# Attention scores on 64 rows of the tensor engine, and the sink as a score column, in a two-layer decoder step

## The chip, the cores and the metric

The program runs on one core of a Trainium2 chip. Times are microseconds (us) of device time for one execution; the time of the kernel is the median of its runs.

## The reference, cut to what matters

One inference step of a two-layer decoder: layer 0 mixes tokens with sliding-window attention, layer 1 with gated linear attention; each is followed by a gated convolutional FFN and a layer norm. 512 prompt positions and 8 single-token samples go through together (520 columns). All arithmetic is float32. The part that the change touches is the prompt's attention of layer 0: 16 query heads, 2 key/value heads (8 query heads share one), head size 64, window 128, and a learned sink per head that takes part in the softmax but has no value:

```
scores = einsum('bnqkgd,bnskd->bnkgqs', qb, kk) * HEAD_DIM ** -0.5   # 128 queries x 256 keys a block
mask   = (kpos >= 0) & (kpos <= qpos) & (qpos - kpos < 128)
s = where(mask, scores, -1e30);  m = maximum(max(s), sink)
p = exp(s - m);  probs = p / (sum(p) + exp(sink - m));  o = probs @ vv
```

## The kernel before, in words

**Layout.** Activations lie with features on the 128 partitions and positions along the free dimension. The 520 positions form two groups, a (positions 0 to 255) and b (256 to 511 and the 8 samples). Work is a list of units, one 128x1024 weight tile each; unit 0 makes the keys, unit 1 the values, units 2 to 9 the queries (unit c+2 holds head c in partitions 0 to 63 and head c+8 in 64 to 127), then come 8 units of the output projection and the FFN. Every unit is done for group a and, some units later, for group b (`order`).

**Float32 in two parts.** TensorE multiplies in fp32r, a shortened float32. So each operand is split in a high part (ScalarE copies it to fp32r) and a low part (VectorE subtracts the high part from the original), and a product is hi*hi + hi*lo + lo*hi: three matmuls for each of 8 chunks (`product`, L164 to L166). Weights arrive by DMA in `raw` (two buffers, RAWS = 2, so a load waits until the low part wl of the load two before it is done, L152); their high part wh is made on GpSimd for the first ten units (L151) and on ScalarE after that (L149).

**Attention, one query unit of one group (`attn_q`).** After the product and the rotation (`rope`, L318 to L324) the queries are split. In `attn_k` and `attn_q` of this kernel the split is laid out for scores of 128 rows: tile `qs` holds for each of the unit's two heads (v = 0, 1) the 64 rows of the high part and, in the other 64 partitions, the 64 rows of the low part (L371, L372, 64 partitions each); the keys' high and low parts are each stored twice, in both halves (`khi[v]`, `klo[v]`, L335 to L339). So one matmul of 128 rows does qhi*khi + qlo*khi (L395) and a second adds the products with klo (L396): 2 matmuls for each head and block of 128 queries, 8 a unit. Scores go to a PSUM tile `sc` per head (two buffers).

The mask keeps for every query the lower triangle of its own block and the upper triangle of the block before, so both fit in one 128x128 square: a predicated copy puts the own block's part over the other one (L408, L412). Group a's first block has no block before it: there VectorE adds mask0 and takes the maximum in one instruction (L406). Then come the maximum (L409, L413), its negative with the sink (L415), exp(sink - m) on ScalarE (L416), the two exponentials with their sums (L418), the sum with the sink's part (L419), its reciprocal (L420), and the scaling by it, on GpSimd for v = 0 and on VectorE for v = 1 (L423). One unit later the probabilities are transposed (L429), copied (L431), split in the two triangles on GpSimd (L435), and again one unit later multiplied with the values (L445; each head takes 64 columns of TensorE).

**Order.** The instruction order of each engine's queue is fixed when the program is built, by a planner that simulates the engines; it starts from the order of the code and lets what its simulation has ready go ahead. Engines run their queues in order. The transfers of the value and key caches (`vc`, `kc`) go out in the same SyncE queue as the weights; the one for `vc` (L380) is pinned behind the weight load that stands before it in the code.

Of the kernel before, what the change touches and what calls it, by code (L numbers as in the profile page):

```python
# [11 lines left out]
F32 = mybir.dt.float32  # L12
F32R = mybir.dt.float32r
I32 = mybir.dt.int32
AF = mybir.ActivationFunctionType
ALU = mybir.AluOpType
AX = mybir.AxisListType
# [3 lines left out]
P = 128  # L21
D = 1024
KD = 8
SEQ = 512
# [12 lines left out]
NEG = -1e30  # L37
# [29 lines left out]
C_SINK = C_LNB + 4 * KD  # L67
# [22 lines left out]
class Net:  # L90
# [175 lines left out]
    def attn_open(self):  # L266
        nc, I = self.nc, self.I
        self.ap, self.ap_cm = self.open("attn")
        p = self.ap
        t = lambda s, name, dt=F32: p.tile(s, dt, name=name)  # L270
        self.rope_t = t([P, 2, NT], "rope_t")
        self.mask0 = t([P, P], "mask0")
        self.own = t([P, 2, P], "own", I32)


        warm = self.acc.tile([P, 512], F32, name="accp")
        for _ in range(WARM):
            nc.tensor.matmul(warm[:, :P], self.ones_c, self.ones_c, start=True, stop=True)
        with self.tc.manual_schedule(engines={mybir.EngineType.SP}):
            r = self.raw.tile([P, KD * P], F32, name="raw")  # L280
            h, l = (self.wts.tile([P, KD * P], F32R, name=n) for n in ("wh", "wl"))
            for m in range(0, KD, 4):
                c = slice(m * P, m * P + 4 * P)
                nc.sync.dma_start(out=r[:, c], in_=I["w_qkv"][0][:, c])
                nc.gpsimd.tensor_scalar(h[:, c], r[:, c], 1.0, 0.0, op0=ALU.mult, op1=ALU.add)
                self.load_x(0, m, m + 2)
                nc.vector.tensor_tensor(l[:, c], r[:, c], h[:, c].bitcast(F32), op=ALU.subtract)
                self.load_x(0, m + 2, m + 4)
            self.w[0] = (h, l)
            self.load_unit(1, 4)  # L290
            nc.sync.dma_start(out=self.par, in_=I["par"])
            nc.sync.dma_start(out=self.rope_t[:, :, 0:256], in_=I["rope"][:, :, 0:256])
            nc.sync.dma_start(out=self.ident, in_=I["ident"])
            self.load_unit(2, 2)
            self.load_unit(3)
            for m in range(0, KD, 4):
                self.load_x(1, m, m + 4)
            nc.sync.dma_start(out=self.rope_t[:, :, 256:], in_=I["rope"][:, :, 256:])
            nc.sync.dma_start(out=self.mask0, in_=I["mask"])
            nc.sync.dma_start(out=self.own, in_=I["own"])  # L300
            for i in range(4, WSLOTS):
                self.load_unit(i)
        self.bq = t([P, KD], "bq")
        nc.vector.tensor_scalar(self.bq, self.par[:, C_BQKV + 2:C_BQKV + 10], 0.125, None, op0=ALU.mult)
        self.khi = [t([P, SEQ], f"khi{v}", F32R) for v in range(2)]
        self.klo = [t([P, SEQ], f"klo{v}", F32R) for v in range(2)]
        self.vtok = t([P, 4, P], "vtok")
        self.kc = t([P, NS, P], "kc")
        self.vc = t([P, NS, P], "vc")
        self.qz = t([P, NS * P], "qz")  # L310
        nc.gpsimd.memset(self.qz, 0.0)
# [15 lines left out]
    def attn_k(self, g, u):  # L327
        nc = self.nc
        ps = self.product(g, u, g.xh, g.xl)
        r = self.rope(g, ps, 1.0, self.par[:, C_BQKV:C_BQKV + 1])  # L330
        cs = slice(g.c0, g.c0 + 256)
        for v in range(2):
            own = slice(64 * v, 64 * v + 64)
            oth = slice(64 - 64 * v, 128 - 64 * v)
            nc.scalar.activation(self.khi[v][own, cs], r[own, :256], AF.Copy)  # L335
            nc.scalar.activation(self.khi[v][oth, cs], r[own, :256], AF.Copy)
            hi = self.khi[v][own, cs].bitcast(F32)
            nc.vector.tensor_tensor(self.klo[v][own, cs], r[own, :256], hi, op=ALU.subtract)
            nc.vector.tensor_tensor(self.klo[v][oth, cs], r[own, :256], hi, op=ALU.subtract)  # L339
        yield 0  # L340
        if g.i:
            self.pcopy(self.kc[:, :, 127], r[:, 256:])
            nc.scalar.dma_start(out=self.O["k_prompt"], in_=r[:, 128:256])
# [19 lines left out]
    def attn_q(self, g, u, c):  # L363
        nc = self.nc
        ps = self.product(g, u, g.xh, g.xl)
        r = self.rope(g, ps, 0.125, self.bq[:, c:c + 1])
        qs = self.ap.tile([P, 2, 256], F32R, name="qs", bufs=2)
        for v in range(2):
            own = slice(64 * v, 64 * v + 64)
            oth = slice(64 - 64 * v, 128 - 64 * v)  # L370
            nc.scalar.activation(qs[own, v], r[own, :256], AF.Copy)  # L371
            nc.vector.tensor_tensor(qs[oth, v], r[own, :256], qs[own, v].bitcast(F32), op=ALU.subtract)  # L372
            if g.i:
                o = c + 8 * v
                self.pcopy(self.qz[own, o:o + 7 * 144 + 1:144], r[own, 256:])
        if g.i and c < 2:
# [7 lines left out]
        yield 1  # L384


        parts = []
        scs = [self.mtile("sc").rearrange("p (b w k) -> p b w k", b=2, w=2) for v in range(2)]
        for v in range(2):
            for b in range(2):  # L390
                n = 2 * g.i + b
                keys = slice(0, 256) if n == 0 else slice(P * (n - 1), P * (n + 1))
                o = scs[v][:, b].rearrange("p w k -> p (w k)")
                qb = qs[:, v, b * P:(b + 1) * P]
                nc.tensor.matmul(o, qb, self.khi[v][:, keys], start=True, stop=False)  # L395
                nc.tensor.matmul(o, qb, self.klo[v][:, keys], start=False, stop=True)  # L396
        prs = []
        for v in range(2):
            h = c + 8 * v
            sink = self.par[:, C_SINK + h:C_SINK + h + 1]  # L400
            sc = scs[v]
            pr = self.ap.tile([P, 2, P], F32, name="pr", bufs=4)
            small = self.ap.tile([P, 8], F32, name="small", bufs=4)
            mx, nm, es, den = (small[:, 2 * i:2 * i + 2] for i in range(4))
            if g.i == 0:
                nc.vector.tensor_tensor_reduce(pr[:, 0], sc[:, 0, 0], self.mask0, 1.0, NEG,  # L406
                                               op0=ALU.add, op1=ALU.max, accum_out=mx[:, 0:1])
                nc.vector.copy_predicated(sc[:, 1, 0], self.own[:, 0], sc[:, 1, 1])  # L408
                nc.vector.tensor_reduce(mx[:, 1:2], sc[:, 1, 0], axis=AX.X, op=ALU.max)  # L409
                src = [pr[:, 0], sc[:, 1, 0]]  # L410
            else:
                nc.vector.copy_predicated(sc[:, :, 0], self.own, sc[:, :, 1])  # L412
                nc.vector.tensor_reduce(mx, sc[:, :, 0], axis=AX.X, op=ALU.max)  # L413
                src = [sc[:, 0, 0], sc[:, 1, 0]]
            nc.vector.tensor_scalar(nm, mx, sink, -1.0, op0=ALU.max, op1=ALU.mult)  # L415
            nc.scalar.activation(es, nm, AF.Exp, bias=sink)  # L416
            for b in range(2):
                nc.scalar.activation(pr[:, b], src[b], AF.Exp, bias=nm[:, b:b + 1], accum_out=den[:, b:b + 1])  # L418
            nc.vector.tensor_tensor(den, den, es, op=ALU.add)  # L419
            nc.vector.reciprocal(den, den)  # L420
            for b in range(2):
                eng = nc.vector if v else nc.gpsimd
                eng.tensor_scalar(pr[:, b], pr[:, b], den[:, b:b + 1], 1.0, op0=ALU.mult, op1=ALU.mult)  # L423
            prs.append(pr)
        yield 1
        for pr in prs:
            tp = self.mtile("tp")[:, :256]
            for b in range(2):
                nc.tensor.transpose(tp[:, b * P:(b + 1) * P], pr[:, b], self.ident)  # L429
            pt = self.ap.tile([P, 2, P], F32, name="pt", bufs=2)  # L430
            nc.scalar.copy(pt.rearrange("p b q -> p (b q)"), tp)  # L431
            pu = self.ap.tile([P, 2, P], F32, name="pu", bufs=2)
            pl = self.ap.tile([P, 2, P], F32, name="pl", bufs=2)
            for dst, sgn, base in ((pu, 1, 0), (pl, -1, -1)):
                nc.gpsimd.affine_select(out=dst, in_=pt, pattern=[[0, 2], [sgn, P]], compare_op=ALU.is_ge,  # L435
                                        fill=0.0, base=base, channel_multiplier=-sgn)
            parts.append((pl, pu))
        yield 1
        pv = self.mtile("pv")
        for b in range(2):  # L440
            n = 2 * g.i + b
# [597 lines left out]
```

## Time and profile before

| | us |
|---|---|
| median of 3 runs (1185.88 to 1188.42) | 1185.92 |
| the profiled execution | 1187.92 |
| its span | 1185.1 |
| PE busy in the span | 1127.1 (95%) |
| VectorE busy | 777.6 (66%) |
| ScalarE busy | 556.0 (47%) |
| GpSimd busy | 362.0 (31%) |

In the profile PE is TensorE's matmuls and PEld its weight loads, DVE is VectorE, ACT ScalarE, POOL GpSimd, SP SyncE (SPq its queue of DMA issues). Matmuls are pipelined: a row's duration is longer than the distance to the next one, and a busy PE is not one at its peak. A float32 matmul that isn't fp32r shows as two rows. PEclk is the granted share of TensorE's full clock. An arrow names what ended a wait.

### The profile page before, as it was taken

How to read it: one execution, taken by the hardware profiler on the slowest of the kernel's cores; microseconds unless marked ns; L12 is line 12 of the kernel's file. 1: busy time of each engine (PE TensorE's matmuls, PEld its weight loads, DVE VectorE, ACT ScalarE, POOL GpSimd, SP SyncE). 2: the span in 40 equal slices, each digit the busy share in tenths (PEclk: the TensorE clock that was granted, in tenths of full speed). 3: DMA queues.
4: the chain of work that ended last, by engine and by line, in shares of the span. 5: the costliest groups of instructions: out<-in, count | busy, mean ns of one | idle time of the engine just before them, and what ended most of it. 6: DMA issues, size and time to landing. Idle time of an engine off the chain costs nothing.

```text
span 1185.1 us, 24433 instructions
## 1 busy us (share of the span) xinstructions
PE 1127.1 (95%) x9598; PEld 1088.0 (92%) x9598; DVE 777.6 (66%) x1649; ACT 556.0 (47%) x1222; POOL 362.0 (31%) x603
## 2 busy tenths in 40 slices
PE   8869989999999999999899999998999999999994
PEld 7768779899999999999799899898999999999994
DVE  7969878854555445558867678789645555355567
ACT  4447645643444234435555455456533443244433
POOL 5646676510011001147500000368210111011345
PEclk9989999999999999999899999999999999999997
DMA  7124013223323232332123553542323332323212
GB/s 224 58 82 138 2 27 123 72 81 116 108 90 108 90 107 90 107 118 95 54 72 95 160 174 121 169 127 90 94 85 119 95 107 90 107 90 107 73 61 72
DMA packets 49547, 118.57 MB, mean 100 GB/s; under 512 B 5753, under 2 KB 23321, under 8 KB 49433
## 3 DMA queue, kind: packets, MB, share of 16 engines
q1 hardware_dynamic: 47417, 115.41, 31.2%
q10 hardware_dynamic: 2016, 1.62, 0.4%
q8 instruction: 75, 1.23, 0.4%
q14 instruction: 39, 0.32, 0.1%
HBM read 108.54 MB, written 8.47 MB: 99 GB/s over the span
## 4 chain that ended last, share of the span: by engine, by line
PE 73%; DVE 12%; DMA 5%; POOL 4%; issue 3%; ACT 2%; SPq 0%; POOLq 0%; DVEq 0%; ACTq 0%
PE accp L165 22%; PE accp L164 22%; PE accp L166 22%; DMA raw<-in_w_qkv 2%; DMA vb<-dv 2%; DVE wl L152 2%; POOL x_b L254 1%; PE pv L445 1%; POOL x_a L254 1%; DVE u L245 1%; DVE qs L372 1%; DVE x_b L240 1%; DVE x_a L240 1%; PE sc L706 1%; PE pv L717 1%
## 5 line engine op out<-in xcount | busy, mean ns | idle before, releaser
L152 DVE TENSOR_TENSOR wl<-raw,wh 128x1024 fp32r<-128x1024 f32 (+2 forms) x189 | 229.1, 1213 | 142.1 <-ACT wh L149 131.6
L149 ACT ACTIVATE wh<-raw 128x1024 fp32r<-128x1024 f32 (+1 forms) x176 | 183.4, 1042 | 215.3 <-PE accp L165 191.8
L164 PE MATMUL accp<-xh_b,wh 128*128 128x264 f32 x976 | 273.5, 280 | 2.8 <-DVE hprod L543 2.8
L165 PE MATMUL accp<-xl_a,wh 128*128 128x256 f32 x976 | 271.4, 279 | 3.5 <-DVE xl_a L257 2.8
L166 PE MATMUL accp<-xh_a,wl 128*128 128x256 f32 x976 | 270.5, 278 | 3.0 <-DVE wl L152 3.0
L165 PE MATMUL accp<-xl_b,wh 128*128 128x264 f32 x976 | 272.8, 280 | 0.4 <-DVE xl_b L257 0.4
L164 PE MATMUL accp<-xh_a,wh 128*128 128x256 f32 x976 | 270.1, 279 | 3.2 <-ACT conv L526 1.4
L166 PE MATMUL accp<-xh_b,wl 128*128 128x264 f32 x976 | 272.1, 279 | 0.0
L165 PEld LDWEIGHTS accp<-xl_a,wh 128*128 128x128 f32 x976 | 187.7, 192 | 5.7 <-DVE xl_a L257 3.7
L164 PEld LDWEIGHTS accp<-xh_a,wh 128*128 128x128 f32 x976 | 187.1, 193 | 6.3 <-ACT conv L526 1.8
L166 PEld LDWEIGHTS accp<-xh_a,wl 128*128 128x128 f32 x976 | 188.1, 193 | 5.0 <-DVE wl L152 4.0
L164 PEld LDWEIGHTS accp<-xh_b,wh 128*128 128x128 f32 x976 | 186.7, 191 | 4.0 <-DVE hprod L543 3.2
L165 PEld LDWEIGHTS accp<-xl_b,wh 128*128 128x128 f32 x976 | 186.6, 191 | 1.9 <-issue 0.9
L166 PEld LDWEIGHTS accp<-xh_b,wl 128*128 128x128 f32 x976 | 186.1, 191 | 1.4 <-issue 1.3
L164 PE MATMUL accp<-hh_b,wh 128*128 128x264 f32 x480 | 133.4, 278 | 2.6 <-ACT hh_b L170 2.6
L165 PE MATMUL accp<-hl_b,wh 128*128 128x264 f32 x480 | 134.2, 280 | 0.0
L166 PE MATMUL accp<-hh_b,wl 128*128 128x264 f32 x480 | 133.3, 278 | 0.0
L165 PE MATMUL accp<-hl_a,wh 128*128 128x256 f32 x480 | 132.3, 276 | 0.3 <-DVE hl_a L171 0.3
L164 PE MATMUL accp<-hh_a,wh 128*128 128x256 f32 x480 | 132.2, 278 | 0.0
L166 PE MATMUL accp<-hh_a,wl 128*128 128x256 f32 x480 | 131.8, 275 | 0.0
L164 PEld LDWEIGHTS accp<-hh_b,wh 128*128 128x128 f32 x480 | 91.2, 190 | 3.1 <-ACT hh_b L170 2.9
L165 PEld LDWEIGHTS accp<-hl_a,wh 128*128 128x128 f32 x480 | 91.9, 192 | 1.3 <-issue 0.8
(304 smaller groups left out, 2095.6 us busy)
## 6 DMA issues: line engine op xcount, KB each, us to landing
raw<-in_w_up SPq DMA_DIRECT2D x88, 512.0 KB, 3.4
raw<-in_w_down SPq DMA_DIRECT2D x32, 512.0 KB, 3.5
raw<-in_w_gla SPq DMA_DIRECT2D x24, 512.0 KB, 3.5
raw<-in_w_mix_o SPq DMA_DIRECT2D x16, 512.0 KB, 3.9
raw<-in_w_down SPq DMA_DIRECT2D x16, 384.0 KB, 3.1
sgla<-in_state_gla SPq DMA_DIRECT2D x16, 256.0 KB, 2.8
vb<-dv SPq DMA_DIRECT2D x16, 256.0 KB, 3.9
out_gla_s<-sgla SPq DMA_DIRECT2D x16, 256.0 KB, 2.9
```

The costliest lines, as they stand in the source:

```text
L149: nc.scalar.activation(h[:, c], r[:, c], AF.Copy)
L152: nc.vector.tensor_tensor(l[:, c], r[:, c], h[:, c].bitcast(F32), op=ALU.subtract)
L164: nc.tensor.matmul(o, h[:, ks], xh, start=k == 0, stop=False)
L165: nc.tensor.matmul(o, h[:, ks], xl, start=False, stop=False)
L166: nc.tensor.matmul(o, l[:, ks], xh, start=False, stop=k == nt - 1)
L240: nc.vector.tensor_tensor(x[:, m], x[:, m], mu, op=ALU.subtract)
L245: nc.vector.tensor_tensor(u, x[:, m], r, op=ALU.mult)
L254: ts = nc.gpsimd.tensor_scalar(x[:, m], u, sc, bi, op0=ALU.mult, op1=ALU.add)
L372: nc.vector.tensor_tensor(qs[oth, v], r[own, :256], qs[own, v].bitcast(F32), op=ALU.subtract)
L445: nc.tensor.matmul(pv[64 * v:64 * v + 64, b * P:(b + 1) * P], self.vtok[:, kb, 64 * v:64 * v + 64], parts[v][w][:, b], start=i == 0, stop= ...
L706: nc.tensor.matmul(up, vks[b][:, 0:P], vks[b][:, P:], start=True, stop=True)
L717: nc.tensor.matmul(ob, att[:, b], vks[b][:, P:], start=first, stop=True)
```

## The change

Keys and queries are split in the plain way, 128 partitions at a time, and the keys are stored once. A score is now three matmuls of 64 rows, qhi*khi + qlo*khi + qhi*klo, where head v uses the partitions of its own half; the two heads of a unit alternate, each into its own `sc` tile. That is 12 matmuls a unit in place of 8. The sink's value is written by VectorE into the column behind the 128 masked scores, so that the maximum (now one instruction that also negates) and the exponentials with their sums take it in; the separate steps for it go. In group a's first block the mask is put in by a predicated copy in place of the add-and-maximum. The scaling of v = 1 becomes one instruction for both blocks.

```diff
-        self.khi = [t([P, SEQ], f"khi{v}", F32R) for v in range(2)]
-        self.klo = [t([P, SEQ], f"klo{v}", F32R) for v in range(2)]
+        self.khi = t([P, SEQ], "khi", F32R)
+        self.klo = t([P, SEQ], "klo", F32R)
 # attn_k
-        for v in range(2):
-            own = slice(64 * v, 64 * v + 64)
-            oth = slice(64 - 64 * v, 128 - 64 * v)
-            nc.scalar.activation(self.khi[v][own, cs], r[own, :256], AF.Copy)
-            nc.scalar.activation(self.khi[v][oth, cs], r[own, :256], AF.Copy)
-            hi = self.khi[v][own, cs].bitcast(F32)
-            nc.vector.tensor_tensor(self.klo[v][own, cs], r[own, :256], hi, op=ALU.subtract)
-            nc.vector.tensor_tensor(self.klo[v][oth, cs], r[own, :256], hi, op=ALU.subtract)
+        self.split(self.khi[:, cs], self.klo[:, cs], r[:, :256])
 # attn_q
-            nc.scalar.activation(qs[own, v], r[own, :256], AF.Copy)
-            nc.vector.tensor_tensor(qs[oth, v], r[own, :256], qs[own, v].bitcast(F32), op=ALU.subtract)
+        self.split(qh, ql, r[:, :256])
...
-                nc.tensor.matmul(o, qb, self.khi[v][:, keys], start=True, stop=False)
-                nc.tensor.matmul(o, qb, self.klo[v][:, keys], start=False, stop=True)
+            for i, (q, k) in enumerate(((qh, self.khi), (ql, self.khi), (qh, self.klo))):
+                for v in range(2):
+                    own = slice(64 * v, 64 * v + 64)
+                    nc.tensor.matmul(scs[v][:, b], q[own, b * P:(b + 1) * P], k[own, keys], start=i == 0, stop=i == 2)
...
-                nc.vector.tensor_tensor_reduce(pr[:, 0], sc[:, 0, 0], self.mask0, 1.0, NEG,
-                                               op0=ALU.add, op1=ALU.max, accum_out=mx[:, 0:1])
-                nc.vector.copy_predicated(sc[:, 1, 0], self.own[:, 0], sc[:, 1, 1])
-                nc.vector.tensor_reduce(mx[:, 1:2], sc[:, 1, 0], axis=AX.X, op=ALU.max)
+                nc.vector.copy_predicated(sc[:, 0, 0:P], self.mask0.bitcast(I32), self.mask0)
+                nc.vector.copy_predicated(sc[:, 1, 0:P], self.own[:, 0], sc[:, 1, P:])
             else:
-                nc.vector.copy_predicated(sc[:, :, 0], self.own, sc[:, :, 1])
-                nc.vector.tensor_reduce(mx, sc[:, :, 0], axis=AX.X, op=ALU.max)
-            nc.vector.tensor_scalar(nm, mx, sink, -1.0, op0=ALU.max, op1=ALU.mult)
-            nc.scalar.activation(es, nm, AF.Exp, bias=sink)
+                nc.vector.copy_predicated(sc[:, :, 0:P], self.own, sc[:, :, P:])
+            nc.vector.tensor_copy(sc[:, :, P], self.par[:, C_SINK + h:C_SINK + h + 1].broadcast_to([P, 2]))
+            nc.vector.tensor_reduce(nm, sc[:, :, 0:P + 1], axis=AX.X, op=ALU.max, negate=True)
             for b in range(2):
-                nc.scalar.activation(pr[:, b], src[b], AF.Exp, bias=nm[:, b:b + 1], accum_out=den[:, b:b + 1])
-            nc.vector.tensor_tensor(den, den, es, op=ALU.add)
+                nc.scalar.activation(pr[:, b, 0:P + 1], sc[:, b, 0:P + 1], AF.Exp, bias=nm[:, b:b + 1], accum_out=den[:, b:b + 1])
             nc.vector.reciprocal(den, den)
-            for b in range(2):
-                eng = nc.vector if v else nc.gpsimd
-                eng.tensor_scalar(pr[:, b], pr[:, b], den[:, b:b + 1], 1.0, op0=ALU.mult, op1=ALU.mult)
+            if v:
+                nc.vector.tensor_tensor(pr[:, :, 0:P], pr[:, :, 0:P], den.unsqueeze(2).broadcast_to([P, 2, P]), op=ALU.mult)
+            else:
+                for b in range(2):
+                    nc.gpsimd.tensor_scalar(pr[:, b, 0:P], pr[:, b, 0:P], den[:, b:b + 1], 1.0, op0=ALU.mult, op1=ALU.mult)
```

## Rows read from the trace of the kernel before

**Rows 1.** Windows: stretch; PE, PEld, DVE, ACT, POOL busy (instructions); clock, DMA, GB/s.

```profile
15.00:36.00 21.00, 18.09 (x149) 17.25 (x150) 20.69 (x35) 9.78 (x25) 12.50 (x12) 1.00 0.56 180
...
60.00:71.00 11.00, 2.57 (x22) 2.33 (x21) 1.87 (x8) 2.29 (x9) 2.14 (x5) 0.84 0.33 107
...
78.00:102.00 24.00, 24.00 (x209) 22.50 (x208) 21.00 (x64) 16.02 (x47) 13.68 (x24) 1.00 0.50 155
102.00:150.00 48.00, 44.39 (x378) 37.27 (x376) 42.59 (x151) 33.29 (x134) 29.16 (x73) 1.00 0.08 24
150.00:162.80 12.80, 10.03 (x84) 8.03 (x83) 10.58 (x33) 6.83 (x27) 11.23 (x21) 1.00 0.00 0
...
73.50:162.80 89.30, 82.92 (x686) 72.29 (x685) 78.47 (x261) 59.22 (x218) 56.92 (x122) 0.98 0.19 60
```

**Rows 2.** Waits from 59 to 74 us: us in total, times, longest.

```profile
POOL wh L151 <- DMA raw<-in_w_qkv: 8.9, 1, 8.9
...
PE pv L445 <- POOL pu L435: 8.6, 1, 8.6
```

**Rows 3.** Timeline of SyncE's queue: start, us, line, transfer.

```profile
35.98 0.33 SPq L147 DMA_DIRECT2D raw<-in_w_qkv  x1
36.36 0.33 SPq L380 DMA_DIRECT2D vc<-in_cache_v  x1
...
45.05 18.50 SPq L147 DMA_DIRECT2D raw<-in_w_qkv  x1
```

**Rows 4.** Timeline of VectorE ahead of that transfer: start, us, line, instruction.

```profile
16.12 1.17 DVE L339 TENSOR_TENSOR klo<-rr,khi 64x256 fp32r<-64x256 f32 x1
...
27.88 2.02 DVE L372 TENSOR_TENSOR qs<-rr,qs 64x256 fp32r<-64x256 f32 x2
```

**Rows 5.** Timeline of GpSimd in the same stretch.

```profile
32.07 1.25 POOL L151 TENSOR_SCALAR wh<-raw 128x1024 fp32r<-128x1024 f32 x1
```

**Rows 6.** VectorE's groups by line from 73.5 to 162.8 us: count, busy us, mean ns.

```profile
L372 DVE TENSOR_TENSOR qs<-rr,qs 64x256 fp32r<-64x256 f32 x21 | 9.1, 435 | 0.7
L423 DVE TENSOR_SCALAR pr<-pr,small 128x128 f32<-128x128 f32 x26 | 8.6, 372 | 0.4
L415 DVE TENSOR_SCALAR small<-small,par 128x2 f32<-128x2 f32 x26 | 8.5, 332 | 0.3
...
L419 DVE TENSOR_TENSOR small<-small 128x2 f32<-128x2 f32 x26 | 7.2, 275 | 1.8 <-ACT pr L418 1.4
L413 DVE TENSOR_REDUCE small<-sc 128x2 f32<-128x256 f32 x16 | 6.7, 420 | 0.4
...
L171 DVE TENSOR_TENSOR hl_a<-pv,hh_a 128x256 fp32r<-128x256 f32 x7 | 2.9, 409 | 0.0
...
L409 DVE TENSOR_REDUCE small<-sc 128x1 f32<-128x128 f32 x10 | 2.7, 282 | 0.1
```

**Rows 7.** Timeline of TensorE: two neighbouring score matmuls.

```profile
144.19 0.28 PE L395 MATMUL sc<-khi,qs 128*128 128x256 f32 x1
144.31 0.28 PE L396 MATMUL sc<-klo,qs 128*128 128x256 f32 x1
```

**Rows 8.** Timeline of TensorE: two value matmuls on 64 columns each.

```profile
141.49 0.32 PE L445 MATMUL pv<-pl,vtok 128*64 128x128 f32 x1
141.49 0.32 PE L445 MATMUL pv<-pu,vtok 128*64 128x128 f32 x1
```

**Rows 9.** Timeline of TensorE: layer 1's matmul on 64 rows, and what follows.

```profile
676.99 0.70 PE L620 MATMUL sc<-z_a,wa 64*128 64x256 f32 x2
677.62 0.38 PE L164 MATMUL accp<-xh_a,wh 128*128 128x256 f32 x1
677.83 0.28 PE L165 MATMUL accp<-xl_a,wh 128*128 128x256 f32 x1
677.94 0.28 PE L166 MATMUL accp<-xh_a,wl 128*128 128x256 f32 x1
```

**Rows 10.** TensorE's waits from 25 to 160 us: us in total, times, longest.

```profile
PE sc L395 <- ACT pr L418: 5.6, 5, 3.4
```

More of the change, by code (lines that the diff above doesn't have):

```diff
@@ L366, in attn_q @@
         r = self.rope(g, ps, 0.125, self.bq[:, c:c + 1])
[L367 to L370, printed above, removed]
-            nc.scalar.activation(qs[own, v], r[own, :256], AF.Copy)
-            nc.vector.tensor_tensor(qs[oth, v], r[own, :256], qs[own, v].bitcast(F32), op=ALU.subtract)
-            if g.i:
+        qh, ql = (self.ap.tile([P, 256], F32R, name=name, bufs=2) for name in ("qh", "ql"))
+        self.split(qh, ql, r[:, :256])
+        if g.i:
+            for v in range(2):
+                own = slice(64 * v, 64 * v + 64)
                 o = c + 8 * v
@@ L387, in attn_q @@
         parts = []
-        scs = [self.mtile("sc").rearrange("p (b w k) -> p b w k", b=2, w=2) for v in range(2)]
-        for v in range(2):
-            for b in range(2):
[L391 to L394, printed above, removed]
-                nc.tensor.matmul(o, qb, self.khi[v][:, keys], start=True, stop=False)
-                nc.tensor.matmul(o, qb, self.klo[v][:, keys], start=False, stop=True)
+        scs = [self.mtile("sc").rearrange("p (b k) -> p b k", b=2) for v in range(2)]
+        for b in range(2):
+            n = 2 * g.i + b
+            keys = slice(0, 256) if n == 0 else slice(P * (n - 1), P * (n + 1))
+            for i, (q, k) in enumerate(((qh, self.khi), (ql, self.khi), (qh, self.klo))):
+                for v in range(2):
+                    own = slice(64 * v, 64 * v + 64)
+                    nc.tensor.matmul(scs[v][:, b], q[own, b * P:(b + 1) * P], k[own, keys], start=i == 0, stop=i == 2)
         prs = []
@@ L399, in attn_q @@
             h = c + 8 * v
-            sink = self.par[:, C_SINK + h:C_SINK + h + 1]
             sc = scs[v]
-            pr = self.ap.tile([P, 2, P], F32, name="pr", bufs=4)
-            small = self.ap.tile([P, 8], F32, name="small", bufs=4)
-            mx, nm, es, den = (small[:, 2 * i:2 * i + 2] for i in range(4))
+            pr = self.ap.tile([P, 2, P + 2], F32, name="pr", bufs=4)
+            small = self.ap.tile([P, 4], F32, name="small", bufs=4)
+            nm, den = small[:, 0:2], small[:, 2:4]
@@ L405, in attn_q @@
             if g.i == 0:
-                nc.vector.tensor_tensor_reduce(pr[:, 0], sc[:, 0, 0], self.mask0, 1.0, NEG,
-                                               op0=ALU.add, op1=ALU.max, accum_out=mx[:, 0:1])
-                nc.vector.copy_predicated(sc[:, 1, 0], self.own[:, 0], sc[:, 1, 1])
-                nc.vector.tensor_reduce(mx[:, 1:2], sc[:, 1, 0], axis=AX.X, op=ALU.max)
-                src = [pr[:, 0], sc[:, 1, 0]]
-            else:
-                nc.vector.copy_predicated(sc[:, :, 0], self.own, sc[:, :, 1])
-                nc.vector.tensor_reduce(mx, sc[:, :, 0], axis=AX.X, op=ALU.max)
-                src = [sc[:, 0, 0], sc[:, 1, 0]]
@@ L417, in attn_q @@
+            nc.vector.tensor_reduce(nm, sc[:, :, 0:P + 1], axis=AX.X, op=ALU.max, negate=True)
             for b in range(2):
-                nc.scalar.activation(pr[:, b], src[b], AF.Exp, bias=nm[:, b:b + 1], accum_out=den[:, b:b + 1])
-            nc.vector.tensor_tensor(den, den, es, op=ALU.add)
+                nc.scalar.activation(pr[:, b, 0:P + 1], sc[:, b, 0:P + 1], AF.Exp, bias=nm[:, b:b + 1], accum_out=den[:, b:b + 1])
             nc.vector.reciprocal(den, den)
-            for b in range(2):
-                eng = nc.vector if v else nc.gpsimd
-                eng.tensor_scalar(pr[:, b], pr[:, b], den[:, b:b + 1], 1.0, op0=ALU.mult, op1=ALU.mult)
+            if v:
+                nc.vector.tensor_tensor(pr[:, :, 0:P], pr[:, :, 0:P], den.unsqueeze(2).broadcast_to([P, 2, P]), op=ALU.mult)
+            else:
+                for b in range(2):
+                    nc.gpsimd.tensor_scalar(pr[:, b, 0:P], pr[:, b, 0:P], den[:, b:b + 1], 1.0, op0=ALU.mult, op1=ALU.mult)
@@ L428, in attn_q @@
             for b in range(2):
-                nc.tensor.transpose(tp[:, b * P:(b + 1) * P], pr[:, b], self.ident)
+                nc.tensor.transpose(tp[:, b * P:(b + 1) * P], pr[:, b, 0:P], self.ident)
             pt = self.ap.tile([P, 2, P], F32, name="pt", bufs=2)
```

## The prediction

> **What bounds the kernel now.** I read the page's busy shares first (TensorE 95% of the span, so over the whole run it is the bound), then the busy time by stage, because the change touches only the first 165 us. There the picture is another one [rows 1]: from 15 to 36 us VectorE is busy 20.69 of 21.00 us, TensorE 18.09; from 102 to 150 us VectorE 42.59 of 48.00, while TensorE issues 378 matmuls, 7.9 a us. From 78 to 102 us, where TensorE is never idle, it issues 209 in 24.00 us, 8.7 a us. So in most of the attention VectorE sets the pace and TensorE has about a tenth to give. Two stretches are different. From 60 to 71 us nearly everything stands (TensorE busy 2.57 of 11.00). The list of waits says why: GpSimd waits 8.9 us for a weight, and TensorE 8.6 us for a triangle that is queued on GpSimd behind that weight [rows 2]. SyncE's timeline shows the weight's issue held for 18.50 us, from 45.05 to 63.55, behind the value cache that was issued at 36.36, directly after the weight load at 35.98 [rows 3]. The cache transfer drains slowly, and nothing in the change touches that. The end of this stall is therefore tied to the moment at which the value cache goes out. The last stretch, 150 to 162.8 us, belongs to GpSimd: busy 11.23 of 12.80 us, TensorE at 84 matmuls, 6.6 a us [rows 1].
>
> **Before the stall.** The value cache goes out behind the load at 35.98, and that load waits for the low part of an earlier weight, which VectorE makes in its turn. So what VectorE saves before 36 us moves the stall. It saves on the keys: four subtractions of 64 partitions for group a lie between 15.6 and 18.9 us, the longest of 1.17 us [rows 4], and become one of 128 partitions and 256 columns, which took 0.409 us where nothing disturbed it [rows 6]. With 0.42 us for an undisturbed one of the four (as the queries' 0.435 mean [rows 6]), they take 3 x 0.42 + 1.17 = 2.4 us, so 2.0 us goes. It saves on the queries of two units: two subtractions in 2.02 us [rows 4], twice, become two of 0.41 to 1.0 us (the upper end if GpSimd disturbs the wide one as it does the narrow one), so 2.0 to 3.2 us goes. That is 4.0 to 5.2 us of VectorE's time. Not all of it arrives: the weight's high part is made on GpSimd from 32.07 to 33.32 [rows 5], the low part can't start before that, and GpSimd waits in that stretch on VectorE's rotation but also on transfers. Bounds for the shift of the stall: 0 (GpSimd and the transfers set it) and 5.2 us (VectorE alone sets it). With VectorE 98% busy there I take 3 us. The work of the units between 36 and 60 us gets shorter too, by some 1.2 us a unit (below, 15.3 us over 13 units), but it only runs sooner into the same stall, and this part I cost at nothing. It would be worth something only if the planner moved the value cache or took the weight's high part out of the way of the triangles.
>
> **After the stall, VectorE.** In 73.5 to 162.8 us VectorE is busy 78.47 us [rows 1]. From its groups [rows 6]: L415 goes, 8.5 us. L419 goes, 7.2 us. Of L372's 21 instructions, 9.1 us, half remain at 0.41 us, so 4.8 us goes. Added is one copy of two columns for each of 26 heads: the trace doesn't show it on PSUM; it lies between nothing (hidden in the gap before the next instruction) and the 0.275 us of the 128x2 addition; I take 0.2 us, 5.2 us in all. Group a's heads swap a masked add-and-maximum and a 128-column maximum (0.282 us) for a predicated copy and a 256-column maximum (0.420 us): about even, 0.1 us a head either way. The scaling of v = 1, 13 pairs at 8.6/13 = 0.66 us, becomes one pass over 256 columns at 0.41 us, at best 3.3 us less; undisturbed it may be none. So VectorE loses 8.5 + 7.2 + 4.8 - 5.2 = 15.3 us, up to 18.6, and stands at 60 to 63 us of 89.3. It is no longer what is late.
>
> **After the stall, TensorE.** What is late next is TensorE, and at the end GpSimd. Score matmuls start 0.12 us apart [rows 7], so a unit's 8 cost 0.96 us now. The 12 of the new form cost 6 x 0.12 = 0.72 us if two heads on different rows run together, or 12 x 0.12 = 1.44 us if not. The trace has no two matmuls on different rows side by side; the nearest is the value product, where two matmuls on different columns start at the same hundredth, 141.49 [rows 8]. I go by it: together. To that comes the change of shape. Layer 1's matmul on 64 rows is two passes and the next matmul starts 0.63 us after it, and the one after that 0.21 us later, where a plain neighbour comes after 0.11 [rows 9]. If each pass takes twice the 0.11 us of an fp32r pass of as many columns, this leaves 0.63 - 0.44 = 0.19, and 0.10 behind it: about 0.3 us for going there and back. So a unit costs 0.72 + 0.3 = 1.02 us, against 0.96: 0.06 us more, some 1 us over the 12 units that are still to come after the stall, if the scores stay in one piece. Two pieces cost 0.3 us more each time.
>
> A rule speaks against the change here: the Trainium skill, TensorEngine Tiling (Array Packing), Key Properties, says that changing the tiling mode, not only the tile, drains the engine; the 0.19 and 0.10 us above agree with it. The same skill, TensorE: Matmul & The Clock Gate, Part 3, says that matmuls on distinct row groups run together; no run here shows it on rows, and by it the sum would be the one that I use, by its opposite that of the second rival.
>
> What VectorE's freedom is worth is TensorE's reserve: 378 matmuls at 8.7 a us are 43.4 us instead of 48.0, so 4.6 us from 102 to 150. From 78 to 102 us TensorE has no idle time and VectorE was at 21.00 of 24.00; I allow 1 us. The last 12.8 us are GpSimd's work, which the change leaves as it is, but some of it starts sooner: 1 us. Less 1 us for the shape changes, this part gives 5.6 us. Its bounds: 0 (each unit waits for something else) and 12 us (89.3 us for 686 matmuls, at 8.7 a us throughout 78.9, and some more in the tail).
>
> **The sum.** 3 + 5.6 = 8.6 us. From the profiled execution's 1187.92 (span 1185.1 and 2.8 around it) this gives 1179.3. That execution is 2.0 us above the median of the runs, so on the scale of the median I forecast 1177.3 us. From 170 us on, everything only moves to the left.
>
> **Rivals.** (1) The order that the planner finds shrinks the stall as well, for instance since the triangles get ahead of the weight on GpSimd: up to 8.6 us more, 1168.7. For it: all durations ahead of that place change. Against: the value cache stays pinned behind the same load, and both go in one queue.
>
> (2) Two heads on different rows don't run together. Then a unit costs 1.44 + 0.3 = 1.74 us of TensorE instead of 0.96, 0.78 more, 9.4 us over 12 units: the reserve is eaten, 1177.3 + 9.4 - 1 = 1185.7, no change. For it: the only matmul on 64 rows [rows 9] stands alone. Against: the columns' pairs [rows 8].
>
> (3) Slower: both score tiles are now taken at once. Before, v = 0's four matmuls needed one free `sc` buffer and v = 1's the other, so the first head's scores could run while the second head's exponentials of the unit before were still reading. Now the second matmul in TensorE's queue needs the second buffer, and behind it stand all products. TensorE already waits there, 5 times for 5.6 us in all, 1.1 us each [rows 10]. If all 16 units wait that long, it is 16 x 1.12 - 5.6 = 12.3 us more, 1189.6. It turns the sign from 8.6/16 = 0.54 us a unit on, and the planner hides it where it finds products to run in between. Against it: VectorE's chain on each head is two instructions shorter.
>
> (4) Only the smaller half arrives: the stall's end doesn't move (GpSimd and transfers set it), and of the rest half: 2.8 us, 1183.1.
>
> **How the numbers follow.** A change of less than 0.3%, 3.6 us, can't be told from none. Forecast 0.50, its own range 1171 to 1182 (the shift of the stall between 0 and 5.2, the rest between 4 and 9). Rival 1 0.10, rival 2 0.12, rival 3 0.13, rival 4 0.15. Faster: the forecast, rival 1 and a part of rivals 2 and 4, 0.68. Same: most of rivals 2 and 4, a little of the forecast and of rival 3, 0.20. Slower: rival 3, 0.12. The range goes to rival 1 below and just short of rival 3 above: 1168 to 1188.
>
> **What the profile of the changed kernel would show.** Right: VectorE's busy time before 165 us lower by some 20 to 25 us; the cache transfer's issue at 31 to 34 us instead of 36.36, and TensorE's long wait ending by as much sooner; score matmuls of the two heads starting in pairs, 6 x 0.12 us a unit; the end of the attention 7 to 10 us sooner, and equal distances after it. Wrong: pairs 0.12 us apart one by one (rival 2), waits of the first score matmuls for exponentials of more than 10 us in all (rival 3), the cache's issue still at 36 us (rival 4), or a stall of another length or at another place (rival 1).

## The result, and the profile after

The changed kernel takes 1190.34 us (median of 11 runs, 1186.59 to 1192.31) against 1187.09 for the kernel before (median of 11, 1185.88 to 1188.42): ratio 1.0026, 95% interval 1.0017 to 1.0036. It is a little slower, by 3.1 us (1187.09 x 0.0026); the forecast was 8.6 us faster.

The profiled execution of the changed kernel is the shortest of its runs: 1186.59 us, span 1184.9. The busy times of its page, first line (share of the span, instructions):

```profile
PE 1139.3 (96%) x9662; PEld 1095.6 (92%) x9662; DVE 755.4 (64%) x1563; ACT 540.2 (46%) x1168; POOL 362.6 (31%) x603
```

VectorE lost 22.2 us (777.6 before), TensorE gained 12.2 (1127.1). Nearly all of this lies in the attention. The windows of the changed kernel, with the columns and stretches of [rows 1]:

```profile
60.00:71.00 11.00, 8.86 (x70) 7.57 (x68) 4.70 (x14) 2.44 (x11) 3.72 (x5) 1.00 0.38 114
78.00:102.00 24.00, 24.00 (x197) 20.76 (x196) 19.55 (x55) 13.73 (x45) 17.42 (x36) 1.00 0.27 84
102.00:150.00 48.00, 48.00 (x380) 40.10 (x380) 27.95 (x88) 22.85 (x86) 22.73 (x55) 1.00 0.10 32
...
73.50:162.80 89.30, 83.48 (x664) 70.30 (x662) 58.16 (x170) 44.78 (x157) 55.24 (x112) 1.00 0.18 54
```

From 102 to 150 us VectorE fell from 42.59 to 27.95 us, and ScalarE and GpSimd fell too. But TensorE is now busy in all of the 48.00 us, and it issued 380 matmuls there where it had issued 378. The freed engines had nobody to serve faster.

What keeps it busy is in its timeline. This is one visit to the scores between two products (start, duration, line, tile, rows x columns of the weight):

```profile
102.42 0.28 PE L166 MATMUL accp<-xh_b,wl 128*128 128x264 f32 x1
102.62 0.38 PE L388 MATMUL sc<-khi,qh 64*128 64x256 f32 x1
102.84 0.28 PE L388 MATMUL sc<-khi,ql 64*128 64x256 f32 x1
...
103.31 0.27 PE L388 MATMUL sc<-klo,qh 64*128 64x256 f32 x1
103.52 0.38 PE L164 MATMUL accp<-xh_b,wh 128*128 128x264 f32 x1
103.73 0.28 PE L165 MATMUL accp<-xl_b,wh 128*128 128x264 f32 x1
```

The six follow each other in the order of one head (khi with qh, khi with ql, klo with qh, then the same for the second block), one by one, 0.12 us apart. The next visit to the scores starts at 106.41. The code alternates the two heads, but the built order doesn't: the planner let one head's six go ahead and the other head's six follow some us later. That holds for 13 of the 16 units. From 102.42 to 103.73 are 1.31 us; two neighbouring products would take 0.22, so the visit costs 1.09: 6 x 0.12 for the matmuls and 0.38 for changing shape there and back. The chain of work that ended last in 100 to 150 us, summed by line, puts TensorE's scores first:

```profile
by line: PE sc L388 24.6%; PE pv L432 20.6%; PE accp L165 15.0%; PE accp L164 14.4%; PE accp L166 12.6%; PE tp L416 8.4%; PE sc L442 4.4%; ACT hh_b L170 0.8%; issue 0.0%
```

In the very first unit most of the matmuls of the two heads do stand together, and there the same timeline shows them in pairs, two records on one line (x2) and the next two 0.11 us later:

```profile
25.21 0.29 PE L388 MATMUL sc<-klo,qh 64*128 64x256 f32 x2
25.32 0.28 PE L388 MATMUL sc<-khi,qh 64*128 64x256 f32 x2
```

The stall of 60 to 71 us shrank. SyncE's timeline, then a wait from 59 to 74 us (answering to [rows 3] and [rows 2]), then the end of TensorE's long wait, before and after (in brackets how long it waited, and for what):

```profile
33.92 0.33 SPq L371 DMA_DIRECT2D vc<-in_cache_v  x1
41.27 19.84 SPq L147 DMA_DIRECT2D raw<-in_w_qkv  x1
```

```profile
POOL wh L151 <- DMA raw<-in_w_qkv: 8.2, 1, 8.2
```

```profile
71.13 0.48 PE L445 MATMUL pv<-pu,vtok 128*64 128x128 f32 x1 [8.56 <-POOL pu L435]
```

```profile
71.42 0.44 PE L416 MATMUL tp<-ident,pr 128*128 128x128 f32 x2 [2.56 <-DVE vs L353]
```

The value cache goes out 2.4 us sooner, GpSimd's weight starts at 67.20 instead of 69.67, and TensorE waits 2.6 us instead of 8.6. But its wait doesn't end sooner: it begins 6.3 us later, at 68.86 instead of 62.57 us, and ends at 71.42 instead of 71.13, released by another step, a copy on VectorE. That is 6 us less of waiting, and still the first gate of the FFN, which marks the end of the attention, starts at 210.9 us, against 209.3 before. These are its rows, before (all 88 of them) and after (the first five; shortest, median and longest ns, first and last start):

```profile
L526 ACT ACTIVATE conv<-accp,par x88: 547/572/590, 209.3 to 1129.9; 128x256 f32<-128x256 f32 x88
```

```profile
L513 ACT ACTIVATE conv<-accp,par x5: 555/578/584, 210.9 to 227.7; 128x256 f32<-128x256 f32 x5
```

### The profile page after: what moved, and what is told of

Same layout as the page of the kernel before. It is cut to its first block, busy times and chain, and to the rows that moved or that the text cites. A ratio compares the mean times of both kernels' runs of the same rounds, so it can differ in the third digit from the quotient of the medians.

```text
span 1184.9 us, 24407 instructions
## 1 busy us (share of the span) xinstructions
PE 1139.3 (96%) x9662; PEld 1095.6 (92%) x9662; DVE 755.4 (64%) x1563; ACT 540.2 (46%) x1168; POOL 362.6 (31%) x603
## 3 DMA queue, kind: packets, MB, share of 16 engines
q10 hardware_dynamic: 2016, 1.62, 0.4%
## 4 chain that ended last, share of the span: by engine, by line
PE 76%; DVE 10%; DMA 5%; POOL 4%; issue 3%; ACT 1%; SPq 0%; POOLq 0%; DVEq 0%; ACTq 0%
PE accp L165 23%; PE accp L164 23%; PE accp L166 23%; DMA raw<-in_w_qkv 2%; DMA vb<-dv 2%; PE sc L388 2%; DVE wl L152 2%; PE pv L432 1%; POOL x_b L254 1%; POOL x_a L254 1%; DVE u L245 1%; DVE x_a L240 1%; DVE x_b L240 1%; PE sc L693 1%; DVE msq L235 1%
```

## The experiments

Each ratio is to the kernel before, run on the same chip in the same batch (its median was 1187.0 to 1187.5).

**The new softmax alone**, with the splits and 128-row scores of the kernel before (the edit against the changed kernel, cut to the scores):

```diff
-            for i, (q, k) in enumerate(((qh, self.khi), (ql, self.khi), (qh, self.klo))):
-                for v in range(2):
-                    nc.tensor.matmul(scs[v][:, b], q[own, ...], k[own, keys], start=i == 0, stop=i == 2)
+                nc.tensor.matmul(o, qb, self.khi[v][:, keys], start=True, stop=False)
+                nc.tensor.matmul(o, qb, self.klo[v][:, keys], start=False, stop=True)
```

> The kernel before with its scores on 128 rows and its old splits, and only the softmax of the change (sink as a column, one maximum, one scaling). Theory A (the scores on 64 rows cost TensorE what VectorE gives back: about 1.1 us for each block of six against 0.48 for four before, two blocks a unit): without them the gain shows, 4 to 8 us less than before, ratio 0.993 to 0.997, VectorE busy before 165 us lower by about 15 us and TensorE as before. Theory B (VectorE's freed time is worth nothing, since the stall behind the value cache and GpSimd set the end): ratio 1.000, the end of the attention where it was.

Measured: 1183.38 us, ratio 0.9965 (0.9953 to 0.9977). The window of 102 to 150 us:

```profile
102.00:150.00 48.00, 45.14 (x388) 37.92 (x390) 38.71 (x123) 31.75 (x120) 33.15 (x77) 1.00 0.06 20
```

VectorE 3.9 us lower than before, ten matmuls more in the same time, the gate at 205.9 us. In the whole execution VectorE lost 7.4 us (770.2), half of the 15 that I had expected. This half of the change is a gain of 4.1 us, in the range of theory A.

**The 64-row scores and the plain splits alone**, with the softmax of the kernel before (the difference from the changed kernel, cut to the sink):

```diff
-            nc.vector.tensor_copy(sc[:, :, P], self.par[:, C_SINK + h:C_SINK + h + 1].broadcast_to([P, 2]))
-            nc.vector.tensor_reduce(nm, sc[:, :, 0:P + 1], axis=AX.X, op=ALU.max, negate=True)
+            nc.vector.tensor_scalar(nm, mx, sink, -1.0, op0=ALU.max, op1=ALU.mult)
+            nc.scalar.activation(es, nm, AF.Exp, bias=sink)
```

> The change's splits and scores on 64 rows with the softmax of before. Theory A: TensorE pays the 1.2 us a unit (some 19 us in all, part of it hidden in the stall) and VectorE only gets the splits' 8 us back: slower than before by 3 to 8 us, ratio 1.003 to 1.007. Theory B: ratio 1.000 to 1.002, about as the change itself.

Measured: 1188.7 us, 1.0014 (1.0005 to 1.0023), a loss, but a smaller one than theory A wanted; the ratio lies in the range of theory B. VectorE lost 13.9 us in the whole execution (763.7). TensorE is nearly full in the window, although VectorE has more to do than in the changed kernel:

```profile
102.00:150.00 48.00, 47.47 (x385) 39.73 (x383) 33.08 (x113) 26.17 (x104) 23.86 (x59) 1.00 0.10 34
```

The halves don't add: -4.1 and +1.7 (1187.5 x 0.0014) would be -2.4, and the whole is +3.1. With the 64-row scores TensorE is nearly full already, so the lighter softmax, which gains 4.1 us without them, gains nothing with them.

**The alternation held in TensorE's queue.** The changed kernel, with the score matmuls of a unit kept in the order of the code:

```diff
-                    nc.tensor.matmul(scs[v][:, b], q[own, b * P:(b + 1) * P], k[own, keys], start=i == 0, stop=i == 2)
+                    mm = nc.tensor.matmul(scs[v][:, b], q[own, b * P:(b + 1) * P], k[own, keys], start=i == 0, stop=i == 2)
+                    if b or i or v:
+                        self.tc.keep_in_program_order(mm)
```

> The changed kernel with its score matmuls pinned in the order of the code, so that the two heads really alternate in TensorE's queue. Theory A: twelve matmuls take six steps of 0.12 us and the change of shape is paid once a unit, so 1.1 to 1.3 us a unit instead of 2.2; 4 to 9 us less than the changed kernel, ratio to before 0.994 to 0.999. Rival: pairing doesn't help because both score tiles must now be free before TensorE goes on; waits of the scores for exponentials of more than 10 us, and a time like the change's or longer.

Measured: 1181.24 us, 0.9959 (0.9946 to 0.9971). Its timeline has the pairs:

```profile
126.51 0.44 PE L418 MATMUL tp<-ident,pr 128*128 128x128 f32 x2
126.88 0.39 PE L388 MATMUL sc<-khi,qh 64*128 64x256 f32 x2
127.10 0.28 PE L388 MATMUL sc<-khi,ql 64*128 64x256 f32 x2
...
127.57 0.28 PE L388 MATMUL sc<-klo,qh 64*128 64x256 f32 x2
127.78 0.44 PE L418 MATMUL tp<-ident,pr 128*128 128x128 f32 x2
```

Twelve matmuls go where six went. This unit stands whole, as only 3 of the 16 do; in half of them the planner let one matmul go ahead of the other eleven, and then a unit takes two visits, of 0.52 and 1.10 us. In 102 to 150 us TensorE issued 415, 96 of them scores, against 380 with 78 (both counted by line); so 319 others instead of 302:

```profile
102.00:150.00 48.00, 46.37 (x415) 37.32 (x414) 31.25 (x106) 26.09 (x102) 28.11 (x65) 1.00 0.08 24
```

The gate moves from 210.9 to 202.4 us, 8.5 us, and the whole time by 9.1. From 25 to 160 us the scores wait for exponentials of the unit before for 0.2 us in all, not for more than 10, so the rival of the expectation is out. The order of the score matmuls is all that differs in the code (the planner then places the rest anew), so the loss of the change lies there.

**The changed kernel again**, unaltered, since its profiled execution had been its shortest run:

> The changed kernel once more, unaltered, for a second profile: its runs spread from 1186.6 to 1192.3 and the profiled one was the shortest. If TensorE's clock at the short stops after the stall is what makes the difference, a profile of a longer run shows a lower granted clock in 68 to 80 us and is 3 to 4 us longer from there; ratio 1.002 to 1.004.

Measured: 1190.24 us, 1.0028 (1.0017 to 1.0039), span 1190.0. The granted clock was lower for a while after the stall, part of the time at the lower of its levels (1.2 and 2.4 GHz). TensorE had waited 3.41 us there, up to 72.29, against 2.56 us, up to 71.42, in the first profile. The window, here and in the first profile, and in the kernel before, where TensorE had waited 8.56 us:

```profile
71.00:78.00 7.00, 5.71 (x33) 5.42 (x34) 5.56 (x17) 3.81 (x13) 5.36 (x10) 0.76 0.71 206
```

```profile
71.00:78.00 7.00, 5.49 (x43) 5.00 (x44) 5.18 (x18) 4.14 (x14) 5.44 (x10) 1.00 0.81 238
```

```profile
71.00:78.00 7.00, 6.23 (x32) 5.50 (x33) 6.77 (x22) 3.08 (x13) 5.36 (x10) 0.52 0.25 75
```

But the gate starts at 211.7 us, only 0.8 later than in the first profile. The other 4.3 us between the two spans arise in layer 1, between its first parts and its last addition (809.6 against 814.7; 809.2 in the kernel before). The first 1.4 of them are the clock there: it stood at the lower level until 595.8 us instead of 592.2 (granted clock 0.66 against 0.77 from 582 to 597 us), and from one group of transposes to the next (L678) TensorE took 5.67 us instead of 4.25. So the clock was lower after the stall, as expected, but cost 0.8 us there and not 3 to 4.

**Three and three.** Is the strict alternation needed, or is it enough that the heads stand together? The order within a block becomes three matmuls of one head, then three of the other:

```diff
-            for i, (q, k) in enumerate(((qh, self.khi), (ql, self.khi), (qh, self.klo))):
-                for v in range(2):
+            for v in range(2):
+                for i, (q, k) in enumerate(((qh, self.khi), (ql, self.khi), (qh, self.klo))):
...
+                    if b or i or v:
+                        self.tc.keep_in_program_order(mm)
```

> The changed kernel with its score matmuls pinned head by head within a block: three of head v = 0, three of v = 1, the same for the second block. So both heads stand together, but don't alternate matmul by matmul. If alternating is what pays (two rows sets share a step only when neighbours in the queue use different rows): most of the twelve take a step of 0.12 us each, 1.4 us and one or two changes of shape, about 1.9 us a unit against 2.2 of the changed kernel and 1.1 of the alternating one; ratio to before 0.999 to 1.002. If standing together is enough, it is as fast as the alternating one, 0.995 to 0.997.

Measured: 1178.26 us, 0.9924 (0.9911 to 0.9936), the opposite of what I held likelier. The timeline of one unit that the planner cut after its first three:

```profile
100.11 0.38 PE L388 MATMUL sc<-khi,qh 64*128 64x256 f32 x1
100.33 0.28 PE L388 MATMUL sc<-khi,ql 64*128 64x256 f32 x1
100.45 0.28 PE L388 MATMUL sc<-klo,qh 64*128 64x256 f32 x1
...
101.19 0.39 PE L388 MATMUL sc<-khi,qh 64*128 64x256 f32 x2
101.41 0.28 PE L388 MATMUL sc<-khi,ql 64*128 64x256 f32 x2
101.53 0.28 PE L388 MATMUL sc<-klo,qh 64*128 64x256 f32 x2
101.65 0.28 PE L388 MATMUL sc<-khi,qh 64*128 64x256 f32 x1
```

The nine that are left take six steps: three of one head run beside three of the other, although those stand three places behind in the queue. So strict alternation isn't needed. But standing together is not enough in every order: one unit of the changed kernel itself stands in one visit, from 32.97 us on, by its rows one head's six and then the other's six. There only three pairs form:

```profile
33.32 0.39 PE L388 MATMUL sc<-khi,qh 64*128 64x256 f32 x2
33.54 0.28 PE L388 MATMUL sc<-khi,ql 64*128 64x256 f32 x2
33.66 0.28 PE L388 MATMUL sc<-klo,qh 64*128 64x256 f32 x2
33.77 0.28 PE L388 MATMUL sc<-khi,qh 64*128 64x256 f32 x1
```

Its twelve take nine steps, and the visit costs 1.45 us instead of 1.10. How far behind a partner may stand was not tried beyond these two orders. That three and three led the alternation by 3 us is not the scores' doing; see the last pair below.

**The cover taken away.** The stall hides part of what TensorE does more. It comes from the value cache's one transfer of 127 partitions, so that transfer is cut in two, here in three kernels and below in two more:

```diff
-                d = nc.sync.dma_start(out=self.vc[0:127], in_=self.I["cache_v"][:, 1:128].rearrange("b s f -> s b f"))
+                d = nc.sync.dma_start(out=self.vc[0:112], in_=self.I["cache_v"][:, 1:113].rearrange("b s f -> s b f"))
+                self.tc.keep_in_program_order(d)
+                d = nc.sync.dma_start(out=self.vc[112:127], in_=self.I["cache_v"][:, 113:128].rearrange("b s f -> s b f"))
```

The kernel before with it:

> The kernel before with only the value cache in two transfers. If the stall hangs on the drain, 4 to 9 us less than before, ratio 0.992 to 0.997, TensorE's wait of 8.6 us gone; VectorE stays the bound of the stages around it. If not, 1.000.

The changed kernel with it:

> The changed kernel with only the value cache in two transfers. In the changed kernel TensorE waits just 2.6 to 3.4 us at the stall, since its longer score work reaches into it. So without the stall it should gain only about that, ratio to before 0.999 to 1.001, and stand behind the kernel before with the same transfers by 6 us or more: the change's cost without the cover. If the stall is not what covers it, it gains as much as the kernel before does.

The alternating kernel with it:

> The alternating kernel with the value cache loaded by two transfers, of 112 and 15 partitions, in place of one of 127. If the stall from 60 to 70 us hangs on the slow drain of that one transfer (27.3 us for 508 KB), TensorE's wait of 7.8 us there goes for the most part: 4 to 8 us less than the alternating kernel, ratio 0.988 to 0.993. If the drain is slow for another reason (many short pieces), nothing changes: 0.996.

Measured, in that order: 1178.05 us, 0.9922 (0.9910 to 0.9935); 1184.25, 0.9969 (0.9956 to 0.9981); 1171.08, 0.9866 (0.9851 to 0.9881). The changed kernel gained 6 us from it, where I had expected 2.6 to 3.4; it stands 6.2 us behind the kernel before with the same transfers, as expected. In the first of the three the next weight's issue is no longer held, and TensorE works through the stretch. SyncE's timeline, then the window:

```profile
45.22 0.36 SPq L147 DMA_DIRECT2D raw<-in_w_qkv  x1
```

```profile
60.00:71.00 11.00, 9.64 (x83) 8.79 (x81) 9.94 (x31) 6.65 (x24) 8.31 (x16) 1.00 0.15 48
```

Without the stall's cover the change costs 6.2 us (1184.25 - 1178.05) instead of 3.1, and the alternating kernel gains 7.0 (1178.05 - 1171.08) instead of 4.9 to 6.2 (by the ratio and by the medians): same signs, and for the change a larger size. A part of these differences is TensorE's clock, which the runs don't separate from the waits: from 15 to 165 us the granted clock was 0.95 in the kernel before with the cut transfer (at the lower level, among others, from 42 to 44 us, after TensorE had waited 3.4 us), 0.97 in the changed and 1.00 in the alternating one.

**What is the best version, and do the 64 rows bring anything in it?** Three and three, and the new softmax alone, both with the cut transfer:

> The kernel with three score matmuls of each head in turn, and the value cache in two transfers. The split cache took 10 us off the alternating kernel and 9 off the kernel before. TensorE waited 5.1 us at the stall in the kernel without the split, so if the gains add, 6 to 10 us less than that one: ratio to before 0.984 to 0.988, the shortest of all. If this kernel's lead over the alternating one (3 us) came only from its order around the stall, the lead goes and it stands at the 0.9866 of the alternating kernel with the split.

> The scores on 128 rows of before, the new softmax, and the value cache in two transfers. If the softmax's 4 us and the cache's 9 us add, ratio 0.988 to 0.990; the scores on 64 rows with both heads together are then worth 2 to 5 us more (splits of 128 partitions on VectorE). If VectorE's freed time only counts where the stall doesn't cover it, more than the sum: 0.984 to 0.988.

Measured: 1170.53 us, 0.9865 (0.9848 to 0.9881), and 1169.91, 0.9858 (0.9843 to 0.9873). Three things follow. Three and three no longer leads the alternation (1170.53 and 1171.08), so its 3 us went with the stall: TensorE had waited 5.1 us there and the alternation 7.8. The new softmax and the cut transfer give more together than apart (17.1 us, and 4.1 + 9.4), as the second case of the expectation said. And the 128-row scores of the kernel before, with the new softmax, are as good as any 64-row version: once most of the two heads' matmuls are paired, the 64 rows neither cost nor bring anything that these runs can tell. The last one beats both kernels, by 17.1 us the one before (1186.97 in its batch). Its window:

```profile
102.00:150.00 48.00, 43.96 (x386) 37.17 (x386) 37.02 (x116) 29.13 (x115) 35.33 (x75) 1.00 0.01 2
```

## Why the prediction was wrong

**Before the stall: the transfers right, TensorE's wait wrong.** The value cache was to go out at 31 to 34 us and went at 33.92; the stall was to move by 3 us, and GpSimd's weight moved by 2.5. But TensorE's wait, which was to end as much sooner, ended 0.3 us later (71.42 against 71.13). Instead TensorE got further before it had to wait, which the prediction had costed at nothing: from 36 to 60 us it was busy 23.13 us instead of 18.37, and from 60 to 71 us 8.86 instead of 2.57.

**VectorE: right.** Before 165 us it was to lose 20 to 25 us and lost 20.9 (134.75 to 113.85). After the stall it was to stand at 60 to 63 us of 89.3 and stands at 58.16, but with fewer heads in that stretch, 20 and not 26, since more units were done ahead of the stall. Its groups from 73.5 to 162.8 us give the terms (count, busy us, mean ns):

```profile
L402 DVE TENSOR_REDUCE small<-sc 128x2 f32<-128x258 f32 x20 | 8.4, 422 | 0.5
L407 DVE TENSOR_TENSOR pr<-pr,small 128x256 f32<-128x256 f32 x11 | 6.1, 557 | 0.1
L400 DVE COPY_PREDICATED sc<-own,sc 128x256 f32<-128x256 int32 x14 | 6.0, 428 | 6.9 <-PE sc L388 6.8
...
L401 DVE COPY sc<-par 128x2 f32<-128x2 f32 x20 | 3.2, 159 | 0.2
```

The copy that I had put at 0.2 us takes 0.159, the scaling 0.557 instead of 0.41. The idle time ahead of L400, 6.9 us, already tells the story: VectorE waits for the scores.

**TensorE: the step that failed.** "So a unit costs 0.72 + 0.3 = 1.02 us" holds "if the scores stay in one piece". They didn't. In 13 of the 16 units the planner cut them between the heads. With that both terms double: nothing runs in pairs, so the matmuls cost 12 x 0.12 = 1.44, and there are at least two visits, so the changes of shape cost 2 x 0.38 = 0.76. Together 2.20 us a unit. The prediction named the price of a second piece (0.3), but gave it no weight and didn't see that it also undoes the pairs. Its own two prices were near: two heads on different rows do run in pairs where they stand near each other, and the change of shape is 0.38 us instead of 0.3. What a visit to the scores adds between its neighbours, from the timelines:

| scores in TensorE's queue | us a visit | us a unit |
|---|---|---|
| before: 4 matmuls of 128 rows, one head | 0.48 | 0.96 |
| after: 6 of 64 rows, one head (median) | 1.10 | 2.20 |
| 12 of both heads, alternating or three and three, unit whole | 1.10 | 1.10 |
| alternating, as half of the units are cut: 1, then 11 | 0.52 and 1.10 | 1.62 |
| three and three, as half of the units are cut: 3, then 9 | 0.75 and 1.10 | 1.85 |

These prices, 0.12 us a step and 0.38 us a visit, account for the times. From 102 to 150 us the changed kernel has 78 score matmuls in 16 visits (three heads are cut once more, in four and two), 15.4 us; the other 302 share 32.6 us, 0.108 each. Before, 69 scores are 8.3 us, and 309 others at that distance 33.4: 41.7 us, so TensorE had some 6 us to give there (the prediction said 4.6), and the scores took 7 us more (15.4 - 8.3). Over all 16 units the timelines of the changed kernel show 35 visits and 180 steps (matmuls that start together are one step): 34.9 us, against 128 x 0.12 = 15.4 before, 19.5 us more. The alternating kernel has 35 visits too, but 110 steps: 26.5 us, 8.4 less than the changed kernel, and its gate is 8.5 us sooner. So what fixing the order saved is the pairs; changes of shape it has as many as the changed kernel.

Where the 19.5 us went shows in TensorE's windows up to the gate, before and after:

```profile
0.00:209.30 209.30, 180.32 (x1442) 162.05 (x1442) 171.31 (x460) 112.45 (x345) 129.84 (x216) 0.97 0.30 95
```

```profile
0.00:210.90 210.90, 194.18 (x1506) 171.11 (x1506) 150.17 (x374) 97.15 (x291) 132.05 (x216) 0.98 0.30 94
```

TensorE is busy 13.9 us more. Of these, 12.3 us filled time in which it had stood idle (29.0 us before, 16.7 after; about half of it in the stall), and 1.6 us made the gate later. The other 5.6 of the 19.5 us are not placed one by one: gaps between matmuls can count as busy, and the clock differs too (from 71 to 78 us 43 matmuls at 1.00 instead of 32 at 0.52).

**The rivals.** (1) did come to pass in that the stall shrank, by 6 us of TensorE's time, and it was no gain: the work that ran ahead there was paid back by dearer scores. (2) is wrong in its reason, since two heads on different rows do run together where they stand near each other, but its price for a unit (1.74 us) points the right way: the pairs were lost, by the order. (3) came nearest in time (1189.6), by luck: in the changed kernel no score matmul waits for exponentials from 25 to 160 us, and one weight load for the scores does, for 0.8 us. (4) holds in a part: the transfers moved and TensorE's wait still ended where it had.

The Trainium skill, TensorE: Matmul & The Clock Gate, Part 3, says that matmuls on distinct row groups overlap; here the pairs at 25.21 and 126.88 us show it on rows. The same skill, TensorEngine Tiling (Array Packing), Key Properties, says that a change of tiling mode drains the engine; the 0.38 us a visit agree.

**What stays open.** The gate was 1.6 us later in one profile and 2.4 in the other. The whole is 3.1 us longer by the ratio, and the rest comes up in layer 1, which the change doesn't touch and which took 4.3 us more in one execution of the same kernel than in the other. The clock accounts for 1.4 of these; what moves the other 3 was not found. The planner's reasons for cutting between the heads weren't looked into either; the runs show only what it costs.

## What to carry to other kernels

A saving on the engine that sets the pace is worth no more than the next engine's reserve, so price what the change adds to that engine in the order that it will really have. Matmuls that pay only as neighbours (here two heads on different rows) must be held together where a planner may move them; here fixing their order was worth 9 us. And look at what makes the longest stall: cutting one odd transfer in two gave more than the whole change was forecast to.

## What the runs showed of the hardware

Pairing doesn't need strict alternation: with three matmuls of one head and then three of the other, twelve in one visit still cost 1.10 us. With six and then six they cost 1.45 us, with only three pairs.

The slow transfer has a rate. This view of the kernel before, from 36 to 64 us in 40 equal slices, is the rate of all transfers in GB/s, and below it is the kernel before with the cache cut:

```profile
GB/s 4 48 205 392 115 20 21 20 19 19 19 19 106 31 18 19 19 19 21 20 19 19 19 31 19 19 18 19 42 19 19 19 19 19 18 19 19 19 19 19
```

```profile
GB/s 0 59 111 380 349 319 255 26 0 0 0 0 53 41 47 187 357 170 0 0 0 0 0 0 12 0 47 135 410 181 0 0 0 0 0 0 0 0 0 0
```

508 KB to 127 partitions drain at 19 GB/s for 27 us (36.36 to 63.55). With the transfer cut into 112 and 15 partitions, issued at 36.54 and 37.21, the traffic is over by 42 us. The Trainium skill, DMA: Bandwidth & Descriptors, "Why a DMA increments its semaphore by 16 and not by 1", says that 127 partitions put a transfer on a single engine. The steady 19 GB/s and the cure agree. So does the busy share of the core's 16 DMA engines while it drains, the last figure but one of this window of the kernel before; one engine of 16 would be 0.06:

```profile
46.00:50.00 4.00, 3.90 (x33) 3.53 (x32) 3.87 (x15) 1.29 (x6) 2.60 (x5) 1.00 0.08 19
```

No row names the engine.
